# First loads over SyncE's hardware queue, uncast, and products that follow each B pair, in a one-core matmul with logsumexp

## The chip, the cores and the metric

The kernel runs on one core of one Trainium2 chip. The metric is the device time of one execution in microseconds (us). The spread between executions of one kernel is about 1 to 2 us, so differences below 1 us need several rounds and an interval.

## The reference

```python
# a: [1024, 4096] f32, b: [4096, 4096] f32
def reference(a, b):
    x = np.matmul(a, b)
    return special.logsumexp(x, axis=-1).astype(np.float32)   # [1024]
```

## The kernel before

The kernel works in f16 with f32 accumulation. It treats B in eight blocks of 512 columns. From the second block on it uses a fast matrix multiplication scheme with sums of tiles; that part is one long row of TensorE work and is not touched. The first block, called the **first stage** here, does three things at once: it loads A in row tiles and B in pairs of k tiles, transposes A on TensorE, and makes plain products for six of the eight row groups. Loads come through GpSimd's software queue, which casts f32 to f16 on the way.

One **round** covers four k tiles (`KN = 4`): six row tiles of A (128x512) and two B pairs (128x2x512). There are eight rounds. "Tile 2" below is the row tile of row group 2, counted from 0; "pair 1" is the second B pair of the first round.

```python
arrivals = []                       # the order of loads, and of use
for k0 in range(0, KT, KN):
    for m in range(MT - 2):
        arrivals.append((k0, KN, "a", m))
        if m < KN // 2:
            arrivals.append((k0 + 2 * m, 2, "b", k0))

def load_a(k0, kn, m):              # GpSimd's queue casts f32 -> f16
    slot = stg_slots[:, loads[0] % NSLOT, 0 : kn * P]
    loads[0] += 1
    nc.gpsimd.dma_start(out=slot, in_=a_m[m, :, k0 * P : (k0 + kn) * P])
    stg[k0, m] = slot
# ... transpose_group: four 128x128 transposes into PSUM, then one copy
#     to SBUF, on DVE for every other group and on ACT for the rest ...
# ... behind(): the products that a landed tile or pair makes possible ...

warm(10)                            # ten products of zeros
coming = list(arrivals)

def load(k0, kn, what, x):
    if what == "a":
        load_a(k0, kn, x)
    else:
        blk0.load(k0 // 2, k0 // 2 + 1)          # nc.gpsimd.dma_start
    if len(coming) == len(arrivals) - 3:
        make_identity(nc, ident)
        # ... two small memsets ...

back = []
for n, (k0, kn, what, x) in enumerate(arrivals):
    while coming and (coming[0][2] == "b" or loads[0] < count[0] + NSLOT):
        load(*coming.pop(0))
        # ... after the last one, the loads of the next block ...
    if what == "a":
        transpose_group(k0, kn, x)
    if k0 < KN and x < 3:
        warm(1)
    if len(back) == min(3, 1 + n // 8):          # products lag 1 to 3 arrivals
        behind(*back.pop(0))
    back.append((k0, kn, what, x))
while back:
    behind(*back.pop(0))
```

Of the kernel before, what the change touches and what calls it, by code (L numbers as in the profile page):

```python
# [13 lines left out]
def kernel(  # L14
# [6 lines left out]
    nc = tc.nc  # L21
    P = 128
    FD = 512
    H = FD // 2
    f32 = mybir.dt.float32
# [14 lines left out]
    a_m = a.rearrange("(p mt) k -> mt p k", mt=MT)  # L40
    KN = 4
# [3 lines left out]
    fix_pool = ctx.enter_context(tc.tile_pool(name="fix", bufs=1))  # L45
# [12 lines left out]
            name=nc.get_next_instruction_name(),  # L58
# [11 lines left out]
    stg_slots = tb.rearrange("p t (i j) n -> p (t i) (j n)", j=4)  # L70
    NSLOT = 3 * KP // 4
# [53 lines left out]
    b_rows = b.rearrange("(i t p) n -> p i t n", p=P, t=2)  # L125

    class Block:
# [9 lines left out]
        def load(self, lo, hi):  # L137
            nc.gpsimd.dma_start(  # L138
                out=self.raw[lo // GI][:, lo % GI : lo % GI + hi - lo],
                in_=b_rows[:, lo:hi, :, ts(self.nb, FD)],  # L140
            )
# [31 lines left out]
    blk0, blk1 = Block(0), Block(1)  # L173
    stg = {}
# [12 lines left out]
    loads = [0]  # L187

    def load_a(k0, kn, m):
# [4 lines that stand above are left out]
# [3 lines left out]
    def transpose_group(k0, kn, m):  # L197
        src = stg.pop((k0, m))
        n = count[0]
        count[0] += 1  # L200
        pst = tps[n % 2]
        for j in range(kn):
            nc.tensor.matmul(  # L203
                pst[:, ts(j, P)],
                src[:, ts(j, P)],
                ident,
                is_transpose=True,
                start=(j == 0),
                stop=(j == kn - 1),
            )  # L210
        dst = aT[:, k0 // 2 : (k0 + kn) // 2, :, m // 2, m % 2, :]
        v = pst[:, 0 : kn * P].rearrange("p (i t c) -> p i t c", t=2, c=P)
        if n % 2 == 0:
            nc.vector.tensor_copy(out=dst, in_=v)  # L214
        else:
            nc.scalar.copy(out=dst, in_=v)  # L216
# [3 lines left out]
    def plain(pt, i, kp, m):  # L220
        nc.tensor.matmul(  # L221
            pt,
            aT[:, i, kp, m // 2, m % 2, :],
            blk0.raw[i // GI][:, i % GI, kp, :],
            start=(done[m] == 0),
            stop=(done[m] == KT - 1),
        )
        done[m] += 1

    def a_sums_early(r, q):  # L230
        a11, a12 = aT[:, r, 0, q, 0, :], aT[:, r, 1, q, 0, :]
        a21, a22 = aT[:, r, 0, q, 1, :], aT[:, r, 1, q, 1, :]
        add(s1[:, r, q], a11, a22)
        add(s2[:, r, q], a21, a22)
        add(s5[:, r, q], a11, a12)

    def a_sums_late(r, q):
        a11, a12 = aT[:, r, 0, q, 0, :], aT[:, r, 1, q, 0, :]
        a21, a22 = aT[:, r, 0, q, 1, :], aT[:, r, 1, q, 1, :]
        sub(a21, a21, a11)  # L240
        sub(a12, a12, a22)

    def first_max(m):
        lse_max(acc[m // 2][m % 2], m, 0)
        lse_exp(acc[m // 2][m % 2], m, 0)

    arrivals = []
# [9 lines left out]
    def behind(k0, kn, what, x):  # L257
        if what == "a":
            have_a.setdefault(k0, []).append(x)
            todo = [(k, x) for k in range(k0, k0 + kn) if k in have_b]  # L260
        else:
            have_b.update({k0: 1, k0 + 1: 1})
            todo = [(k, m) for k in (k0, k0 + 1) for m in have_a.get(x, [])]
        for k, m in todo:
            plain(acc[m // 2][m % 2], k // 2, k % 2, m)
        r = slice(k0 // 2, (k0 + kn) // 2)
        if what == "a":
            if x >= 3 and in_place:
                a_sums_late(*in_place.pop(0))
            if x % 2 == 1 and k0 + kn < KT:  # L270
                a_sums_early(r, x // 2)
            if x == 5:
                in_place.extend([(r, 0), (r, 1), (r, 2)])
            if k0 + kn == KT and x == 4:
                first_max(0)
                first_max(1)
                for what in ("t1", "t6"):
                    blk1.make(what, 0, 2)

    def warm(n):  # L280
        for _ in range(n):
            nc.tensor.matmul(acc[2][1], zeros[:, 0:P], zeros[:, 0:FD], start=True, stop=True)  # L282
# [4 lines left out]

    coming = list(arrivals)

    def load(k0, kn, what, x):  # L290
        if what == "a":
            load_a(k0, kn, x)
        else:
            blk0.load(k0 // 2, k0 // 2 + 1)
        if len(coming) == len(arrivals) - 3:
            make_identity(nc, ident)
            nc.gpsimd.memset(negmax, 3.0e38)
            nc.gpsimd.memset(tsum, 0.0)
# [5 lines that stand above are left out]
            if not coming:  # L304
                for lo in range(0, KP, 2):
                    blk1.load(lo, lo + 2)
# [4 lines that stand above are left out]
        if len(back) == min(3, 1 + n // 8):  # L311
            behind(*back.pop(0))
        back.append((k0, kn, what, x))
    while back:
        behind(*back.pop(0))
    for m in range(2, MT - 2):
# [20 lines left out]
    for step, (_, qs) in enumerate(plan):  # L337
# [4 lines left out]
        if more:  # L342
            if plan[step + 1][0] is again1:
                nxt = last
            else:
                nxt = plan[step + 1][0]()
                if step == 1:
# [3 lines left out]
                        out=ident[0:1, 0:2], in_=aT[0:1, 0, 0, MP - 1, :, 0]  # L351
# [17 lines left out]
        for q in qs:  # L369
# [24 lines left out]
            s = fix_pool.tile([P, 4, H], f32, name=f"s_{step}_{q}", tag="s")  # L394
            x, e = s[:, 1::2], s[:, 0:2]
            if final:
                e = fix_pool.tile([P, 2, H], f32, name="e_last", tag="e")
            if joint and q > 0:
                e = e_next
# [78 lines left out]
            if final:  # L478
# [29 lines left out]
                    out=w, in_=w, func=AF.Exp, bias=n0, scale=-1.0, accum_out=l0  # L508
# [81 lines left out]
```

## Time and profile before

| | before |
|---|---|
| time when the prediction was made, median of 6 | 424.79 us |
| time over all runs of the main comparison, median of 20 | 424.32 us (423.75 to 425.62) |
| span of the profiled execution | 423.3 us (this one took 425.08 us, slower than the median) |
| start of the second stage in the profile | 63.50 us |

Part 2 of the page of the kernel before cuts the span into 40 slices of 10.6 us: a digit is the busy share in tenths, the last line the GB/s that the DMA engines wrote.

```profile
PE   5989999999999999999999999999999999999995
...
DMA  8999999999999499102990069400990039799000
GB/s 115 200 197 193 203 205 207 206 207 215 194 185 200 70 161 207 31 2 33 207 159 2 2 109 208 84 2 2 190 206 4 2 60 207 132 199 198 3 2 0
```

TensorE (PE) has idle time only in the first three slices and in the last. The DMA engines write 115 GB/s in the first slice and about 200 in the next twelve.

The table by windows of the kernel before (columns: the stretch, its length, busy us and instructions of each engine, granted clock, DMA share, GB/s):

```profile
core 0: us, PE busy (x) PEld busy (x) DVE busy (x) ACT busy (x) POOL busy (x), PEclk, DMA share, GB/s
0.00:5.00 5.00, 3.81 (x11) 1.42 (x12) 0.27 (x1) 1.28 (x1) 3.88 (x13) 1.00 0.46 61
5.00:10.00 5.00, 2.48 (x17) 0.96 (x15) 1.12 (x4) 0.59 (x1) 3.58 (x7) 1.00 1.15 159
10.00:15.00 5.00, 4.38 (x33) 2.50 (x34) 1.45 (x5) 1.05 (x2) 3.67 (x7) 1.00 1.22 195
15.00:20.00 5.00, 5.00 (x39) 2.71 (x38) 2.75 (x11) 1.29 (x3) 3.78 (x7) 1.00 1.24 202
20.00:25.00 5.00, 3.75 (x30) 2.05 (x29) 2.56 (x12) 1.17 (x2) 2.40 (x5) 1.00 1.24 203
```

The first 5 us move at 61 GB/s, and the next 5 us at three quarters of the later rate. The GB/s are of bytes written: software loads read twice as much as they write, because they cast.

The timeline of TensorE in the kernel before; the bracket gives the idle time just before the row and what ended it. These are all the gaps over 60 ns between the warm-up and the end of TensorE's work:

```profile
7.58 0.40 PE L203 MATMUL tps_98<-ident,tb 128*128 128x128 f16 x4 [1.79 <-DMA tb<-in_a_dram]
...
10.62 0.40 PE L203 MATMUL tps_97<-ident,tb 128*128 128x128 f16 x4 [1.35 <-DMA tb<-in_a_dram]
...
24.64 0.40 PE L203 MATMUL tps_97<-ident,tb 128*128 128x128 f16 x4 [1.25 <-DMA tb<-in_a_dram]
```

All three wait for a row tile (`tb<-in_a_dram`). They sum to 4.39 us, 1.0% of the time.

### The profile page before, as it was taken

Reading aid. Unit: us, or ns where it says so; the run is one execution under the profiler, and the core shown is the slowest. Engines: PE = TensorE matmul, PEld = TensorE weight load, DVE = VectorE, ACT = ScalarE, POOL = GpSimd, SP = SyncE. Lnnn points to the kernel's source line nnn. Section 1 sums busy time; section 2 is a strip of 40 time slices with the busy share of each in tenths; the row PEclk is TensorE's granted clock in tenths of the full one; section 3 lists DMA queues with packets and bytes.
Section 4 is the critical chain, followed back from the end, with each engine's and each line's share of the span. In section 5 each row is a group of like instructions: output and inputs, shape, how many; then the busy total and the mean of one; then the engine's idle time right before and its main releaser. Section 6 shows DMA issues by size and latency. Waiting matters only on the chain.

```text
span 423.3 us, 8529 instructions
## 1 busy us (share of the span) xinstructions
PE 412.8 (98%) x3647; PEld 348.2 (82%) x3647; DVE 258.6 (61%) x571; ACT 109.3 (26%) x278; POOL 74.3 (18%) x117
## 2 busy tenths in 40 slices
PE   5989999999999999999999999999999999999995
PEld 2545558888888888888888888888888888888884
DVE  1456778979736792357812594336832587299854
ACT  1222232132132221222222212222221222222223
POOL 7767663101001030003000030001200030110000
PEclk9999999999999999999999999999999999999998
DMA  8999999999999499102990069400990039799000
GB/s 115 200 197 193 203 205 207 206 207 215 194 185 200 70 161 207 31 2 33 207 159 2 2 109 208 84 2 2 190 206 4 2 60 207 132 199 198 3 2 0
DMA packets 57845, 52.97 MB, mean 125 GB/s; under 512 B 10192, under 2 KB 57296, under 8 KB 57808
## 3 DMA queue, kind: packets, MB, share of 16 engines
q0 software_dynamic: 49344, 50.34, 72.4%
q1 hardware_dynamic: 8464, 2.10, 3.4%
q8 instruction: 28, 0.46, 0.4%
q14 instruction: 9, 0.07, 0.0%
HBM read 100.66 MB, written 2.10 MB: 243 GB/s over the span
## 4 chain that ended last, share of the span: by engine, by line
PE 94%; DMA 3%; POOL 1%; DVE 1%; ACT 1%; issue 0%; DVEq 0%; ACTq 0%; POOLq 0%
DMA tb<-in_a_dram 3%; PE acc_1_0_1342 L380 2%; PE acc_1_0_764 L380 2%; PE acc_2_0_766 L380 2%; PE acc_0_0_762 L380 2%; PE acc_2_0_4198 L380 2%; PE acc_3_0_3770 L380 2%; PE acc_2_0_3102 L380 2%; PE acc_3_0_2690 L380 2%; PE acc_0_0_2306 L380 2%; PE acc_1_0_1894 L380 2%; PE acc_2_0_1477 L380 2%; PE acc_0_0_3926 L380 2%; PE acc_0_0_3386 L380 2%; PE acc_1_0_2434 L380 2%; PE acc_0_0_1766 L380 2%
## 5 line engine op out<-in xcount | busy, mean ns | idle before, releaser
L380 PEld LDWEIGHTS <-aT 128*128 128x128 f16 x1856 | 181.6, 98 | 21.1
L380 PEld LDWEIGHTS <-s_71 128*128 128x128 f16 x464 | 45.4, 98 | 5.5
L380 PEld LDWEIGHTS <-s_72 128*128 128x128 f16 x464 | 45.4, 98 | 5.2
L380 PEld LDWEIGHTS <-s_73 128*128 128x128 f16 x464 | 45.4, 98 | 5.2
L203 PEld LDWEIGHTS <-tb 128*128 128x128 f16 x192 | 13.9, 98 | 17.4 <-DMA tb<-in_a_dram 11.1
L192 POOL DMA_DIRECT2D tb<-in_a_dram x48 | 26.0, 544 | 6.1 <-issue 2.0
L221 PEld LDWEIGHTS <-aT 128*128 128x128 f16 x192 | 16.8, 98 | 11.9 <-ACT aT L216 0.3
L214 DVE COPY aT<-tps_97 128x512 f16<-128x512 f16 x24 | 10.2, 425 | 25.3 <-PE tps_97 L203 25.1
L216 ACT COPY aT<-tps_98 128x512 f16<-128x512 f16 x24 | 14.0, 585 | 44.8 <-PE tps_98 L203 44.8
L84 DVE TENSOR_TENSOR aT<-aT 128x256 f16<-128x256 f16 (+1 forms) x56 | 16.1, 342 | 0.0
L203 PE MATMUL tps_97<-ident,tb 128*128 128x128 f16 x96 | 9.3, 219 | 2.6 <-DMA tb<-in_a_dram 2.6
L203 PE MATMUL tps_98<-ident,tb 128*128 128x128 f16 x96 | 9.3, 219 | 1.8 <-DMA tb<-in_a_dram 1.8
L81 DVE TENSOR_TENSOR s_71<-aT 128x256 f16<-128x256 f16 (+1 forms) x26 | 8.2, 316 | 3.3 <-ACT aT L216 2.8
L138 POOL DMA_DIRECT2D b_0_2838<-in_b_dram x1 | 0.9, 890 | 45.4 <-PE acc_3_0_2690 L380 45.4
L138 POOL DMA_DIRECT2D b_0_2298<-in_b_dram x1 | 0.9, 878 | 45.4 <-PE acc_3_0_2150 L380 45.4
L138 POOL DMA_DIRECT2D b_0_3378<-in_b_dram x1 | 0.9, 878 | 45.4 <-PE acc_3_0_3230 L380 45.4
L138 POOL DMA_DIRECT2D b_0_3918<-in_b_dram x1 | 0.9, 878 | 45.4 <-PE acc_3_0_3770 L380 45.4
L81 DVE TENSOR_TENSOR s_73<-aT 128x256 f16<-128x256 f16 (+1 forms) x26 | 8.2, 316 | 0.0
L81 DVE TENSOR_TENSOR s_72<-aT 128x256 f16<-128x256 f16 (+1 forms) x26 | 8.2, 316 | 0.0
L138 POOL DMA_DIRECT2D aT<-in_b_dram x4 | 3.5, 898 | 21.2 <-PE acc_1_0_4054 L380 21.2
L282 PE MATMUL acc_1_96<-s_73 128*128 128x512 f16 x15 | 5.7, 508 | 1.2 <-DVE s_73 L285 1.2
L81 DVE TENSOR_TENSOR tb<-aT 128x1024 f16<-128x1024 f16 x8 | 5.2, 687 | 1.0 <-DMA aT<-in_b_dram 1.0
(1047 smaller groups left out, 891.2 us busy)
## 6 DMA issues: line engine op xcount, KB each, us to landing
tb<-in_a_dram POOLq DMA_DIRECT2D x48, 128.0 KB, 5.9
aT<-in_b_dram POOLq DMA_DIRECT2D x4, 1024.0 KB, 15.3
b_0_83<-in_b_dram POOLq DMA_DIRECT2D x4, 256.0 KB, 6.1
b_1_84<-in_b_dram POOLq DMA_DIRECT2D x4, 256.0 KB, 6.7
b_2_85<-in_b_dram POOLq DMA_DIRECT2D x4, 256.0 KB, 6.2
b_3_86<-in_b_dram POOLq DMA_DIRECT2D x4, 256.0 KB, 6.2
b_0_87<-in_b_dram POOLq DMA_DIRECT2D x2, 512.0 KB, 8.6
b_1_88<-in_b_dram POOLq DMA_DIRECT2D x2, 512.0 KB, 11.8
```

Of the source, the lines that this page charges most:

```text
L81: nc.vector.tensor_tensor(out=o, in0=x, in1=y, op=ALU.add)
L84: nc.vector.tensor_tensor(out=o, in0=x, in1=y, op=ALU.subtract)
L138: nc.gpsimd.dma_start(out=self.raw[lo // GI][:, lo % GI : lo % GI + hi - lo], in_=b_rows[:, lo:hi, :, ts(self.nb, FD)],)
L192: nc.gpsimd.dma_start(out=slot, in_=a_m[m, :, k0 * P : (k0 + kn) * P])
L203: nc.tensor.matmul(pst[:, ts(j, P)], src[:, ts(j, P)], ident, is_transpose=True, start=(j == 0), stop=(j == kn - 1),)
L214: nc.vector.tensor_copy(out=dst, in_=v)
L216: nc.scalar.copy(out=dst, in_=v)
L221: nc.tensor.matmul(pt, aT[:, i, kp, m // 2, m % 2, :], blk0.raw[i // GI][:, i % GI, kp, :], start=(done[m] == 0), stop=(done[m] == KT - 1),)
L282: nc.tensor.matmul(acc[2][1], zeros[:, 0:P], zeros[:, 0:FD], start=True, stop=True)
L380: nc.tensor.matmul(c, lhs(i), rhs(i), start=(start and i == 0), stop=(i == KP - 1), skip_group_check=True,)
```

## The change

The intent is to have something to multiply sooner. Row tile 0 and pair 0 come as f32 through SyncE's hardware queue, which is idle at that time, and are cast on DVE and ACT. In the first round, products follow each B pair at once instead of one arrival later. One more thing changes on the side: GpSimd makes the identity matrix (and two small memsets) after the fourth load instead of the third, so pair 1 is issued before it. The cast has to move because the hardware queue does not cast: the Trainium skill, page "DMA: Bandwidth & Descriptors", section "SWDGE vs HWDGE vs iDMA", ties casting in the transfer to GpSimd's queue.

```diff
     coming = list(arrivals)
 
+    def first(k0, kn, what, x):
+        if what == "a":
+            raw = fix_pool.tile([P, FD], f32, name="raw_a", tag="e")
+            slot = stg_slots[:, loads[0] % NSLOT, 0 : kn * P]
+            loads[0] += 1
+            nc.sync.dma_start(out=raw, in_=a_m[x, :, k0 * P : (k0 + kn) * P])
+            nc.vector.tensor_copy(out=slot, in_=raw)
+            stg[k0, x] = slot
+        else:
+            raw = fix_pool.tile([P, 2, FD], f32, name="raw_b", tag="s")
+            nc.sync.dma_start(out=raw, in_=b_rows[:, 0, :, 0:FD])
+            nc.vector.tensor_copy(out=blk0.raw[0][:, 0, 0], in_=raw[:, 0])
+            nc.scalar.copy(out=blk0.raw[0][:, 0, 1], in_=raw[:, 1])
+
     def load(k0, kn, what, x):
-        if what == "a":
+        if len(coming) >= len(arrivals) - 2:
+            first(k0, kn, what, x)
+        elif what == "a":
             load_a(k0, kn, x)
         else:
             blk0.load(k0 // 2, k0 // 2 + 1)
-        if len(coming) == len(arrivals) - 3:
+        if len(coming) == len(arrivals) - 4:
             make_identity(nc, ident)
# ... cut ...
         back.append((k0, kn, what, x))
+        while back and k0 < KN and what == "b":
+            behind(*back.pop(0))
     while back:
```

## The prediction

> **What bounds the kernel now.** The page gives TensorE 98% busy of 423.3 us, granted clock 0.997. The wait view and timeline show four TensorE gaps over 60 ns: 1.20 us at the start, 1.79 us before the second row tile's transposes (7.58), 1.35 us before the third's (10.62), 1.25 us at 24.64. After that TensorE never idles until its last matmul. So the change can give at most the last three, 4.4 us (1.0%).
>
> The first stage (to 63.66 us in the chain of waits) is paced almost equally by TensorE and loads. A round of four k tiles is 24 transposes and 24 products, about 6.5 us in the chain; its loads (six 128 KB row tiles, two 256 KB B pairs, as written) land 6.46 us apart, at 203 to 207 GB/s in the table by windows. A late landing cannot be caught up; an earlier one is kept. The two early gaps are loads: the first two B pairs land about 2.5 us after their predecessors, later ones 1.27, and the windows 0 to 5 and 5 to 10 us move only 61 and 159 GB/s.
>
> **What the change does.** Row tile 0 and B pair 0 leave GpSimd's queue (0.55 to 0.68 us to issue a tile, 0.72 a pair), so the later loads are issued about 1.3 us earlier, until the wait for eight loads in flight binds again. SyncE, idle until then, issues the two f32 loads at about 0.8 us instead of 1.24 and 1.91. The Trainium skill (DMA: Bandwidth & Descriptors, Specifications) gives a first byte after about 0.6 us for the hardware path, 1 us for GpSimd's; this trace shows no plain hardware load. The same page, "Issuing engines are not separate DMA queues", says both run on the same 16 engines: only start and unfilled time are gained, not bandwidth. Added: two DVE casts and one ACT cast of 128x512, estimated 0.4 to 0.6 us each from this trace's 128x512 copies (DVE 0.425, ACT 0.585), in series between landing and first product.
>
> Products of tile 0 with pair 0 now precede tile 1's transposes, and the four products of pair 1 tile 2's; from tile 3 on the order is as before. About 0.9 us of work moves into gaps; none is removed. Warm-up keeps TensorE until about 5.0 us, so tile 0's transposes stay there.
>
> **On the critical path.** I expect tile 2's transposes at about 8.5 us instead of 10.62. TensorE is then 2 to 3 us ahead, but soon waits for loads, whose shift decides: about 0.5 us from the earlier start, 0.3 to 1 us from a fuller queue between 3 and 10 us. The gap at 24.64 (a pair landed 1.3 us late) stays. The first stage ends near 62.1 instead of 63.7 us; the rest is TensorE-bound and passes it on.
>
> **Prediction: 423.2 us** (1.6 us less, 0.4%), 8 in 10 within 421.4 to 424.7. Over 2% faster 1%, within 2% 98%, over 2% slower 1%.
>
> **Right if:** the early gaps shrink from 3.1 us to about 1, small new waits for row tiles appear between 9 and 17 us, the gap near 24 stays, second-stage products start 1 to 2.5 us earlier, and the rest is shifted unchanged. **Wrong if:** TensorE waits long for B's cast (its load landing after 6 us); the two queues slow each other so that tile 1 lands no earlier; or overlapping the first slow pairs hides their whole delay, which would give over 3 us.

## The result, and the profile after

Executions over 1.5% slower than the fastest of the same kernel are left out of the means. The ratios in this document are the mean time of one kernel's runs over that of the other's of the same rounds. So they are not quite the ratio of the medians that are quoted beside them.

| | before | changed |
|---|---|---|
| time, median | 424.32 us (20 runs) | 422.70 us (10 runs, 422.35 to 423.73) |
| ratio, 95% interval | | 0.9959 [0.9948, 0.9970] |
| profiled execution | 425.08 us | 422.35 us |
| second stage starts (profile) | 63.50 us | 60.91 us |
| from there to the end of the span | 359.78 us | 359.66 us |

The change saves about 1.6 us, within the 2% that counts as the same. The two profiled executions differ by 2.7 us, because the profiled one of before was 0.76 us above its median and the other 0.35 us below its own. The last row says where the gain lies: all of it comes before the start of the second stage, and nothing after it moved.

Part 2 of the page of the changed kernel:

```profile
PE   8999999999999999999999999999999999999995
...
DMA  9999999999999199003980089300990049799000
GB/s 185 202 203 204 203 206 207 207 207 215 174 199 211 29 193 207 2 2 49 207 145 2 2 130 208 66 2 2 196 203 3 2 68 207 128 197 202 3 2 0
```

The table by windows of the changed kernel:

```profile
0.00:5.00 5.00, 3.81 (x9) 1.34 (x10) 0.77 (x3) 1.35 (x2) 3.88 (x13) 1.00 0.68 189
5.00:10.00 5.00, 4.75 (x30) 2.34 (x29) 1.65 (x6) 1.14 (x2) 4.50 (x9) 1.00 1.19 179
10.00:15.00 5.00, 4.92 (x39) 2.73 (x36) 2.31 (x9) 1.30 (x3) 3.21 (x6) 1.00 1.22 199
15.00:20.00 5.00, 4.98 (x39) 2.78 (x37) 2.82 (x12) 1.62 (x3) 3.72 (x8) 1.00 1.24 205
20.00:25.00 5.00, 4.65 (x38) 2.48 (x36) 2.92 (x13) 1.45 (x3) 3.19 (x7) 1.00 1.23 201
```

The 189 GB/s have to be read with care, because the two f32 loads write 4 bytes where GpSimd's write 2. The window wrote 0.945 MB, of which the uncast loads are 0.786 MB; counted as f16 they are 0.393 MB, so the window brought 0.55 MB against 0.305 MB before. The difference, 0.25 MB, is 1.2 us at 205 GB/s. The window from 5 to 10 us adds 0.1 MB, another 0.5 us.

The timeline of the changed kernel: SyncE's two issues, the casts, the first product, tile 2's transposes, and the gaps of TensorE over 120 ns in the first 26 us, after the one before warm-up:

```profile
0.74 0.39 SPq L295 DMA_DIRECT2D raw_a<-in_a_dram  x1
...
1.20 0.41 SPq L300 DMA_DIRECT2D raw_b<-in_b_dram  x1
...
3.44 0.43 DVE L296 CAST tb<-raw_a 128x512 f16<-128x512 f32 x1 [2.31 <-DMA raw_a<-in_a_dram]
...
4.93 0.62 ACT L302 CAST b_0_83<-raw_b 128x512 f16<-128x512 f32 x1 [2.90 <-DMA raw_b<-in_b_dram]
4.93 0.43 DVE L301 CAST b_0_83<-raw_b 128x512 f16<-128x512 f32 x1 [1.06 <-DMA raw_b<-in_b_dram]
...
6.59 0.60 PE L221 MATMUL acc_0_91<-b_0_83,aT 128*128 128x512 f16 x2
...
8.10 0.60 PE L221 MATMUL acc_1_92<-b_0_83,aT 128*128 128x512 f16 x2 [0.25 <-ACT aT L216]
...
9.40 0.39 PE L203 MATMUL tps_97<-ident,tb 128*128 128x128 f16 x4
...
21.89 0.40 PE L203 MATMUL tps_97<-ident,tb 128*128 128x128 f16 x4 [0.35 <-DMA tb<-in_a_dram]
```

The three gaps of 1.79, 1.35 and 1.25 us have become 0.25, 0.08 (not shown) and 0.35 us; the first two now end with a copy on ACT or DVE and not with a load. The casts take 0.43 and 0.62 us.

The trace also gives, for each load, when its completion count was full. This table is worked out from it (us; "round 3 tile 2" is the row tile whose landing ends the gap at 24.64 us before and at 21.89 us after):

| landing of | before | changed | order only | uncast by GpSimd | tile only | pair only |
|---|---|---|---|---|---|---|
| tile 0 | 4.29 | 3.42 | 4.32 | 4.30 | 3.46 | 6.13 |
| pair 0 | 6.89 | 4.91 | 6.46 | 5.94 | 6.24 | 4.47 |
| tile 1 | 7.54 | 5.65 | 7.11 | 7.72 | 6.88 | 6.79 |
| pair 1 | 9.95 | 7.41 | 9.73 | 9.06 | 8.98 | 8.46 |
| tile 2 | 10.58 | 8.04 | 10.35 | 9.69 | 9.60 | 9.09 |
| round 3 tile 2 | 24.59 | 21.85 | 24.41 | 23.24 | 23.14 | 22.54 |

In the changed kernel everything lands 2.3 to 2.7 us earlier from pair 1 on. Each column is one execution: "order only" issues the same loads at the same times as the kernel before (within 0.02 us for the first eight), and its pair 0 still landed 0.43 us earlier. A difference of half a microsecond between two columns proves nothing by itself.

### The profile page after: what moved, and what is told of

Read it like the earlier page. It is cut to its first block, busy times and chain, and to the rows that moved or that the text cites. A ratio compares the mean times of both kernels' runs of the same rounds, so it can differ in the third digit from the quotient of the medians.

```text
span 420.6 us, 8536 instructions
## 1 busy us (share of the span) xinstructions
PE 413.8 (98%) x3647; PEld 348.7 (83%) x3647; DVE 259.3 (62%) x573; ACT 110.1 (26%) x279; POOL 73.4 (17%) x115
## 4 chain that ended last, share of the span: by engine, by line
PE 91%; DMA 6%; DVE 1%; issue 1%; ACT 1%; POOL 0%; DVEq 0%; ACTq 0%; POOLq 0%
DMA tb<-in_a_dram 3%; DMA b_0_83<-in_b_dram 3%; PE acc_1_0_1347 L398 2%; PE acc_1_0_769 L398 2%; PE acc_2_0_771 L398 2%; PE acc_2_0_4203 L398 2%; PE acc_3_0_3775 L398 2%; PE acc_2_0_3107 L398 2%; PE acc_3_0_2695 L398 2%; PE acc_0_0_2311 L398 2%; PE acc_1_0_1899 L398 2%; PE acc_2_0_1482 L398 2%; PE acc_0_0_767 L398 2%; PE acc_0_0_3931 L398 2%; PE acc_1_0_3519 L398 2%; PE acc_0_0_3391 L398 2%
```

## The experiments

Two theories are compared. **Theory L**: the landing of the loads decides; the new order of products gains almost nothing. **Rival O**: the order fills TensorE's gaps and brings the gain. Smaller rivals stand with their runs. All runs gave correct results, and all intervals come from five rounds. For each profiled run the table gives the start of the second stage; the span after it was between 359.6 and 360.1 us in all of them, so the first stage alone differs.

| run | median us | ratio [95%] | second stage at us |
|---|---|---|---|
| order only | 424.51 | 1.0001 [0.9988, 1.0013] | 63.13 |
| loads only | 422.55 | 0.9959 [0.9946, 0.9973] | 60.96 |
| uncast by GpSimd | 423.84 | 0.9985 [0.9972, 0.9997] | 62.07 |
| tile only | 423.28 | 0.9976 [0.9964, 0.9989] | 61.87 |
| pair only | 423.07 | 0.9970 [0.9957, 0.9984] | 61.79 |
| cast twice | 422.30 | 0.9957 [0.9945, 0.9970] | 60.98 |
| no fillers | 422.43 | 0.9957 [0.9945, 0.9969] | 60.84 |
| start late by one | 423.88 | 0.9988 [0.9973, 1.0003] | 63.09 |
| start late by three | 427.99 | 1.0089 [1.0074, 1.0103] | 66.59 |
| two of each | 428.30 | 1.0092 [1.0077, 1.0107] | 66.29 |
| two of each, TensorE busy | 426.75 | 1.0053 [1.0041, 1.0065] | 64.93 |
| two of each, late casts | 424.06 | 0.9992 [0.9976, 1.0008] | 63.19 |

### Order only

```diff
 # the kernel before, with
         back.append((k0, kn, what, x))
+        while back and k0 < KN and what == "b":
+            behind(*back.pop(0))
```

> The kernel before with only the new order of products in the first round; all loads stay on GpSimd's queue. Theory L (the landing of the loads decides, the order costs or gains almost nothing): the third row tile and the tile at 24.6 us land when they did, the first product of the second stage stays within 0.4 us of 63.5 us, time 424.3 us (ratio 0.999 to 1.001). Rival O (the order fills the gaps and brings the gain): ratio 0.997 or lower, the second stage starts 1 us or more earlier.

Measured: 1.0001. The gaps in TensorE's timeline of this run show why the order alone is worth nothing (tile names lack their numbers here):

```profile
6.51 0.59 PE L221 MATMUL acc<-b,aT 128*128 128x512 f16 x2 [0.96 <-DMA b<-in_b_dram]
...
9.77 1.02 PE L221 MATMUL acc<-b,aT 128*128 128x512 f16 x4 [0.93 <-DMA b<-in_b_dram]
...
17.44 0.40 PE L203 MATMUL tps<-ident,tb 128*128 128x128 f16 x4 [0.95 <-DMA tb<-in_a_dram]
...
24.45 0.40 PE L203 MATMUL tps<-ident,tb 128*128 128x128 f16 x4 [0.75 <-DMA tb<-in_a_dram]
```

TensorE now waits for the pairs themselves and does some products earlier. What it gained it waits away again at 17.44 and 24.45 us, for row tiles that land when they land. Rival O falls.

### Loads only

```diff
 # the changed kernel, with
-        while back and k0 < KN and what == "b":
-            behind(*back.pop(0))
```

> The changed kernel without the new order: row tile 0 and B pair 0 by SyncE, products behind their loads as before. Theory L: all of the gain, ratio 0.995 to 0.997, the second stage starts at 60.7 to 61.5 us. Rival O: ratio 0.9985 or higher, the second stage starts after 62.5 us.

Measured: 0.9959, the same as the whole change, and the second stage starts at 60.96 us against 60.91. So the loads bring all of the gain that can be resolved.

### Uncast loads by GpSimd

```diff
-            nc.sync.dma_start(out=raw, in_=a_m[x, :, k0 * P : (k0 + kn) * P])
+            nc.gpsimd.dma_start(out=raw, in_=a_m[x, :, k0 * P : (k0 + kn) * P])
-            nc.sync.dma_start(out=raw, in_=b_rows[:, 0, :, 0:FD])
+            nc.gpsimd.dma_start(out=raw, in_=b_rows[:, 0, :, 0:FD])
```

> The changed kernel with the two f32 loads issued by GpSimd instead of SyncE, in the old order of loads; casts as in the change. Theory L with the hardware queue's earlier start and GpSimd's relief as its cause: the gain is gone, ratio 0.9985 to 1.001, the first packet moves at about 2.6 us as before. Rival U (the loads land sooner because they are uncast, whatever the queue): ratio 0.997 or lower, and B pair 0 lands less than 1.8 us after row tile 0.

Measured: 0.9985, on the edge of the first expectation and with an interval just below 1. The first packet moved at 2.66 us, as before. The pair landed 1.64 us after the tile instead of 2.60, as rival U said. But tile 1 behind it landed no earlier (7.72 us against 7.54 before); the gain first shows at pair 1 (9.06 against 9.95). Pair 1 comes with its cast in both kernels, but here it was issued 0.69 us sooner (3.23 us against 3.92), because the identity is made after it. Every run built from the changed kernel has this move of the identity, and no run tests it alone. So the run shows that a part of the gain, by the ratio about a third (0.0015 of 0.0041, with a wide interval), does not need SyncE. Whether this part comes from the missing cast or from the moved identity is not shown.

### Tile only, pair only

```diff
 # tile only
-        if len(coming) >= len(arrivals) - 2:
+        if len(coming) >= len(arrivals) - 1:
 # pair only
-        if len(coming) >= len(arrivals) - 2:
+        if len(coming) == len(arrivals) - 2:
```

> The changed kernel with only row tile 0 by SyncE; B pair 0 stays on GpSimd's queue with its cast. Theory L with an even share for each load: about half of the gain, ratio 0.9972 to 0.9988. If the early start alone matters, nearly all of the gain (0.9965 or lower). If the slow first B pair is what the hardware queue cures, almost none (0.999 or higher). Also: GpSimd's first packets[...] should start at 2.6 us if they waited for nothing but their own issue, and after SyncE's last packet if SyncE's packets go first.

> The changed kernel with only B pair 0 by SyncE; row tile 0 stays on GpSimd's queue with its cast. Tile alone gave 0.9976 and both 0.9959. If the two loads' shares add up, 0.9978 to 0.9988; if the pair, as the larger load and the slow one, carries most, 0.9962 to 0.9975; if only the early start counts, about what the tile alone gave. Row tile 0 should land later than 4.3 us, because SyncE's packets go first, and its transposes start late, at 5.5 us or after, without cost to the total.

Measured: 0.9976 for the tile and 0.9970 for the pair. Each alone gives more than half of 0.9959, so their shares do not add up; the intervals overlap and do not say which is worth more. A share that both runs have, such as something moving from 1.8 us on or the moved identity, would count twice when they are summed; no run separates it. In the run with the pair alone, tile 0 landed only at 6.13 us and its transposes started at 6.18 us after a gap of 0.94 us, as expected without harm to the later loads.

GpSimd's first data packet moved at 2.62 us before, at 2.91 us with the tile on SyncE, at 3.38 us with the pair, and at 4.00 us with both. So neither clean form of the expectation holds: GpSimd's first packet came later the more SyncE carried, but before SyncE's last packet had ended (3.11, 4.12 and 4.60 us).

### Cast twice

```diff
             nc.vector.tensor_copy(out=slot, in_=raw)
+            nc.vector.tensor_copy(out=slot, in_=raw)
# ... and likewise the two casts of the pair, on DVE and on ACT ...
```

> The changed kernel with each of the three casts done twice, the same values written again: 0.43 us more on DVE before the tile's transposes and 0.43 to 0.62 us more before the first product. Theory L: the products are ahead of the loads by more than that at the gap at 22 us, so the time stays, ratio 0.9952 to 0.9968. Rival C (landing, cast and first products in series are the critical path): 0.5 to 1 us longer, ratio 0.9970 to 0.9985.

Measured: 0.9957, no cost. The test was milder than expected. TensorE was busy with its warm-up and began tile 0's transposes at 5.43 us (5.44 in the changed kernel), so the doubled casts moved the first product only from 6.59 to 6.71 us and tile 2's transposes from 9.40 to 9.66. As far as a quarter of a microsecond can tell, the casts are not on the critical path.

### No fillers

```diff
-        if k0 < KN and x < 3:
-            warm(1)
```

> The changed kernel without the five single warm-up products that stand between the first round's transposes (about 1.1 us of TensorE at 0.216 us each); the ten at the start stay. Theory L (in the changed kernel the loads decide from 15 us on): the freed time turns into waits for row tiles, the gap near 22 us grows from 0.35 to about 1 us, the second stage starts at 60.6 to 61.1 us, ratio 0.9950 to 0.9966. Rival P (TensorE's own work from 5.4 us on now paces the first stage, as the two late runs suggest for theirs): about 1 us less, ratio 0.9925 to 0.9945. If the gaps let the clock be halved, slower than the changed kernel.

Measured: 0.9957, second stage at 60.84 us. Taking five products (1.08 us at 0.216 us each) from TensorE between 5.4 and 10 us gains nothing; the timeline of TensorE in this run shows it as waits:

```profile
6.35 0.60 PE L221 MATMUL acc<-b,aT 128*128 128x512 f16 x2 [0.52 <-DVE aT L214]
...
7.86 1.47 PE L221 MATMUL acc<-b,aT 128*128 128x512 f16 x6 [0.68 <-ACT aT L216]
...
10.06 1.04 PE L221 MATMUL acc<-b,aT 128*128 128x512 f16 x4 [0.29 <-DVE aT L214]
...
21.86 0.40 PE L203 MATMUL tps<-ident,tb 128*128 128x128 f16 x4 [0.56 <-DMA tb<-in_a_dram]
```

The row at 21.86 us starts when the same row does in the changed kernel (21.89 us). The row at 10.06 us stands at 10.31 in the changed kernel and at 10.56 with the doubled casts. So in a band of a quarter of a microsecond to either side TensorE's own position does not matter, and in all three kernels the row near 22 us starts 0.04 us after its tile lands.

### Start late, by one write and by three

```diff
# in first(), before the load of the tile; three times in the other run
+            nc.vector.memset(raw, 0.0)
             nc.sync.dma_start(out=raw, in_=a_m[x, :, k0 * P : (k0 + kn) * P])
```

> The changed kernel with three DVE writes of the f32 tile before its load, so that SyncE issues about 1 us later or more; nothing else differs. Theory L says the gain is loads moved in the first 5 us: with the start delayed by 1 us about 0.7 to 1.0 us of the 1.7 us are lost, ratio 0.9975 to 0.9988. Rival (the relief of GpSimd's queue and the pair landing without its slow first touch give the gain, the start does not): ratio 0.9968 or lower. Also: GpSimd's first packet[...] comes at about 2.7 us if it only lost to SyncE's packets, and stays after them if the order of issue decides.

> The changed kernel with one DVE write of the f32 tile before its load: SyncE issues at about 1.8 us instead of 0.74. The run with three writes issued at 3.02 us and let TensorE idle until its clock was halved, so it told nothing of the start alone. Theory L: part of the gain is the start, so 0.4 to 1.2 us are lost, ratio 0.9970 to 0.9988, with no halved clock in the first stage. Rival (start does not matter): 0.9968 or lower.

Measured: 1.0089 with three writes, which neither theory expected, and 0.9988 with one. The run with three issued at 3.02 us, not 1 us late but 2.3, so it is no test of the start. TensorE stood still for 2.69 and 1.85 us, and the record of the granted clock shows half speed from 9.55 us for 6.83 us.

The run with one write issued at 1.70 us. Its profiled execution shows the same thing, shorter: half speed from 8.35 us for 3.41 us, which I had expected not to happen. The table by windows (the granted clock is the third number from the end: 0.57 in the second stretch):

```profile
5.00:8.00 3.00, 1.18 (x8) 0.34 (x6) 0.83 (x3) 0.41 (x1) 2.39 (x4) 1.00 1.18 262
8.00:12.00 4.00, 3.59 (x12) 1.39 (x13) 1.05 (x5) 0.80 (x2) 2.89 (x6) 0.57 1.24 202
12.00:16.00 4.00, 3.92 (x31) 2.21 (x30) 1.45 (x5) 0.86 (x2) 2.66 (x5) 1.00 1.24 201
```

Its six executions fall into two groups: 424.50 to 424.52 us at a mean clock of 0.994 or 0.995, and 423.16 to 423.26 us at 0.997 or 0.999. Only the first was profiled, so that the second ran without a halved clock in the first stage is inferred from its mean clock. The mean is no sure sign: with three writes, one execution with a mean of 1.0 took 428.48 us, as long as two at 0.991 (427.98 and 428.54). If the inference holds, the later start itself costs the difference between 423.2 us and the 422.3 to 422.7 us of the kernels with the early start, 0.5 to 0.9 us of the gain (not more than single executions of one kernel differ), and the halved clock another 1.3 us where it strikes. The landings of the profiled execution point the same way for the start: tile 2 landed at 8.80 us against 8.04 in the changed kernel, and round 3 tile 1 at 19.80 against 19.18. Both runs also put the second-stage start later than the loads explain: with one write, round 3 tile 2 had landed at 21.73 us, no later than in the changed kernel, but TensorE came to it only at 24.41 us. So theory L holds only while TensorE's first work is not late by more than the slack it has.

### Two of each by SyncE

The second tile and pair come by SyncE as well, staged in f32 in the buffers of the next block.

```diff
+            # x == 1: raw = blk1.raw[1][:, 3] seen as f32; likewise pair 1 in blk1.raw[2]
-        if len(coming) >= len(arrivals) - 2:
+        if len(coming) >= len(arrivals) - 4:
             first(k0, kn, what, x)
-        if len(coming) == len(arrivals) - 4:
+        if len(coming) == len(arrivals) - 6:
```

> The changed kernel with row tiles 0 and 1 and B pairs 0 and 1 by SyncE, the second ones staged as f32 in the buffers of the next block. Theory L: the second pair too lands about 1.5 us after its predecessor instead of 1.8 and the next stretch, 5 to 10 us, moves more than 179 GB/s; the first stage ends 0.2 to 0.8 us earlier than in the changed kernel, ratio 0.9940 to 0.9956. Against it: DVE and ACT, in order, cast the second pair before they copy the first transposes, so the first products come about 1 us later; if that decides, ratio 0.996 or higher.

Measured: 1.0092, far worse than either expectation. TensorE's timeline shows one gap, and the table by windows the clock after it:

```profile
10.61 1.04 PE L221 MATMUL acc<-b,aT 128*128 128x512 f16 x2 [3.93 <-DVE aT L214]
```

```profile
5.00:10.00 5.00, 1.68 (x8) 0.72 (x6) 1.02 (x3) 0.79 (x2) 2.89 (x5) 0.97 1.12 247
10.00:15.00 5.00, 4.39 (x14) 1.74 (x15) 1.24 (x5) 0.99 (x2) 2.84 (x5) 0.50 1.23 201
15.00:20.00 5.00, 5.00 (x36) 2.94 (x35) 1.45 (x5) 1.17 (x2) 2.85 (x5) 0.85 1.24 203
```

DVE, which works in order, waited for pair 1 (landed 9.77 us) before it copied the first transposes, so the first product came 4 us late (10.61 us against 6.59). Then the clock was at half speed for 6.83 us (0.50 and 0.85 in the last two stretches). Two follow-ups take these apart.

```diff
# two of each, TensorE busy: 17 more products of zeros in the gap
-            warm(1)
+            warm(18 if n == 1 else 1)
```

> Two row tiles and two B pairs by SyncE, cast early, as in the run that came out at 1.0092, with 17 more warm-up products put into TensorE's 3.9 us gap before its first product. If the halved clock between 9.7 and 16.5 us made that loss (6.83 us at half speed, 3.4 us), the time falls by 2.5 to 3.6 us, ratio 1.0005 to 1.0035, and no halved clock is recorded before the end. If the late first products themselves made it, ratio 1.006 or higher.

Measured: 1.0053, between the two expectations. No halved clock was recorded before the end, and 0.0039 of the 0.0092 (1.7 us) went away. The rest stayed: in this run pair 1 landed 0.85 us later still (10.62 us), and the first product started at 11.46 us.

```diff
# two of each, late casts: the second tile and pair are cast when their turn comes
-            nc.vector.tensor_copy(out=slot, in_=raw)
+            casts[what, k0, x] = lambda: nc.vector.tensor_copy(out=slot, in_=raw)
# ... and likewise for the pair; in the loop over arrivals:
+        if (what, k0, x) in casts:
+            casts.pop((what, k0, x))()
```

> The same four loads by SyncE, but the second tile and pair cast only when TensorE's order comes to them, so that DVE copies the first transposes before it waits for the second pair. Theory L with what the two-each run showed (the two queues alternate from 4 us, so pair 1 lands at about 9.8 us instead of 7.4, while later loads land no earlier than in the changed kernel): no halved clock, no gain over the changed kernel, ratio 0.9955 to 0.9985. If more loads by SyncE still help, 0.9950 or lower.

Measured: 0.9992, just outside the expected range on the slow side; most of the gain is gone though no halved clock was recorded in the first stage. The landing times show the reason. Tile 2 and tile 3, on GpSimd's queue, landed at 6.88 and 9.58 us; tile 1 and pair 1, which are needed first, landed at 8.23 and 11.17 us on SyncE's. Once both queues had work they shared the engines (between 5 and 8 us SyncE's queue moved 0.58 MB of f32 and GpSimd's 0.16 MB of f16, which is 0.31 MB of f32 read), so loads needed later took the time of loads needed now. In the changed kernel pair 1 landed at 7.41 us.

None of the experiments beat the change by more than its interval. The kernels with the loads only, with the casts doubled and without fillers equal it.

## Why the prediction was right

- **The time.** Predicted 423.2 us within 421.4 to 424.7, measured 422.7. The saving of 1.6 us was predicted and is the difference of the medians (by the ratio it is 1.7 us).
- **What bounds the kernel.** "A late landing cannot be caught up; an earlier one is kept" held: the span after the start of the second stage was 359.6 to 360.1 us in all fourteen profiled kernels, and shifts of the first stage between -2.7 and +3.1 us passed on whole.
- **The order moves work and removes none.** Shown by the order alone (1.0001) and the loads alone (0.9959).
- **"The loads' shift decides."** Shown for the changed kernel by the doubled casts and the missing fillers, which move TensorE a quarter of a microsecond to either side and not the time. The landings say it more widely: in the nine profiled kernels in which TensorE waits for round 3 tile 2, that row starts 0.04 or 0.05 us after the landing, and the second stage 38.7 to 39.2 us after the row. It is not a general truth: in the two runs with a late start and the three with two of each, TensorE's first products came so late that they decided.
- **Two terms of the sum.** I gave the earlier start 0.5 us and the fuller queue between 3 and 10 us 0.3 to 1 us. Together that is 0.8 to 1.5 us, less than the 1.6 us that I predicted, so the close hit is partly luck. Divided at 3 us, as in the prediction, and counted as f16, the traces have 0.14 MB more in the changed kernel before 3 us and 0.21 MB more from there to 10 us: 0.7 and 1.0 us at 205 GB/s. Both terms were somewhat small. This counts bytes and does not test causes. The start is not only that SyncE issues half a microsecond sooner than GpSimd; its first packets moved at 1.77 us against 2.62, and then the tile and the pair followed each other at once (3.42 and 4.91 us, against 4.29 and 6.89). By the run with one write, the start's own part is 0.5 to 0.9 us, on the inference told there.
- **What was wrong in detail.** Tile 2's transposes were predicted at about 8.5 us and started at 9.40, because the four products of pair 1 now stand before them; with the loads alone they started at 8.48. The "small new waits for row tiles between 9 and 17 us" did not appear, since loads landed just ahead of TensorE. The gap at 24.64 us did not "stay": it shrank to 0.35 us, because TensorE came to it later relative to the loads; with the loads alone it was 1.03 us, with the same total. The delay of the pair before it did stay (1.28 us before, 1.06 after, against the usual spacing).
- **The profile pair overstates.** The second stage starts 2.59 us earlier in the profile, a little over the predicted 1 to 2.5 us, and the gaps after the first sum to 3.59 us less. The profiled execution of before was a slow one of its kind; and in the changed one the warm-up took longer (its fifteen products averaged 568 ns against 508), which absorbed about 0.9 us of the closed gaps. The records of the granted clock show why: full speed from 6.39 us on, against 4.49 us in the kernel before. Until then the products of zeros start 0.43 us apart, afterwards 0.22. The tables by windows print a clock of 1.00 for this first stretch, for which there is no record.

What stays open: why the first pairs land about 2.5 us after their predecessors on GpSimd's queue with the cast (1.6 us without it), and how the gain divides between the start, the missing cast, GpSimd's shorter queue and the moved identity. Also open is why the pair before the gap at 24.64 us landed 1.3 us late; a fetch of 16 KB of instructions on another queue was in flight then (21.9 us before, 19.5 us in the changed kernel). In all fourteen profiles the first load after 15 us that lands late, by 0.3 to 1.3 us against the usual spacing of 0.65 us for a tile and 1.29 for a pair, lands 1.0 to 1.8 us after such a fetch has ended, though the fetch starts anywhere from 19.5 to 26.3 us. That makes chance unlikely, but no run prevents the fetch, so the cause is not shown. The last row of the landing table carries this delay too.

## What to carry to other kernels

When the first stage is paced by loads, ask when the first bytes move and in which order they land, and move that; here, reordering products around the waits gained nothing. The idle hardware queue was worth using for the very first loads as long as it started before the other queue and carried only what is needed first (0.9959; with the start one write later 0.9988, with four loads and late casts 0.9992). Once two queues ran together they shared the engines without regard to which data are needed next. Early waits of TensorE were followed by a halved clock in three kernels (3.93 us in one wait; 2.69 and 1.85 us; 0.72 and 1.50 us), but not in the kernel before (1.79 and 1.35 us), so check the record of the clock whenever a change makes TensorE wait.

## What the Trainium skill lacked or had wrong

- "DMA: Bandwidth & Descriptors", section "Specifications", gives a first byte after about 0.6 us for the hardware path and 1 us for GpSimd's. From the start of the issuing instruction to the first packet the traces show 1.03 us (0.74 to 1.77) and 1.38 us (1.24 to 2.62). The difference between the two paths, 0.35 us, agrees; both figures are low if counted from there. Counted from the end of the issuing instruction (1.14 and 1.92) the traces show 0.63 and 0.70 us. The section does not say from where it counts.
- The same page, section "Queues, rings and completion order", says that each engine takes its queues in turn, packet by packet. The runs where SyncE started late, or carried four loads, fit this (both queues moved packets in every microsecond from 5 to 8 us). It lacks what these runs show: with SyncE first, GpSimd's first packet moved only at 2.91, 3.38 and 4.00 us (2.62 alone) when SyncE carried 0.26, 0.52 and 0.79 MB; with 1.57 MB it was 4.00 us again (3.94 with late casts).
- The same page, section "Rules for kernel authors", says that spreading loads over issuing engines for bandwidth does not help. The rates agree (from 15 to 25 us 202 and 203 GB/s before, 205 and 201 after), yet two loads moved to SyncE gained 0.4%, through earlier landings. The page does not say that it can also lose: with four loads moved the order of landing was upset and the gain fell to 0.1%, with an interval that includes no gain.
- "TensorE: Matmul & The Clock Gate", section "Part 1: The HAM clock gate", puts the window at 3413 ns and calls it free-running. The records agree to the nanosecond (3413 and 6827 ns at half speed). The first record of full speed starts anywhere from 4.00 to 7.15 us in the fourteen profiles, as a free-running window would have it, and a different phase in each execution would explain why one kernel had two times, 423.2 and 424.5 us (not shown). By these runs such a drop cost 1.3 us for one window, on the inference told above, and 1.7 us for two between two kernels whose landing times also differ.
